# A hybrid SSD and attention encoder step on one core: order of the plain FFN tiles, low parts of three weight pairs by DMA, PSUM banks of the norms in the scan

## The chip, the cores and the metric

The kernel is one program on one core of one Trainium2 chip. The metric is the device time of that core in microseconds, the median of three runs: 2969.83 us before the change (2967.94 to 2970.08). The engines are named as in the profile: PE (TensorE, the matmuls), PEld (its weight loads), DVE (VectorE), ACT (ScalarE), POOL (GpSimd), SP (the queue that issues most DMAs). PSUM is the memory that matmuls write, in banks of 128 x 512 float32; SBUF is the memory that all other operands stand in.

## The reference

Two layers over 1024 prompt frames and 64 frames of a running stream, width 1024. Layer 0 is an SSD scan (Mamba-2) and a SwiGLU FFN, layer 1 band attention and a SwiGLU FFN; every sub-layer has a norm before and after it. Cut to what the change touches:

```python
def rmsnorm(x, w):
    return x * lax.rsqrt(jnp.mean(x * x, axis=-1, keepdims=True) + EPS) * w

def swiglu(u, w_in, w_out):
    g, up = jnp.split(u @ w_in, 2, axis=-1)
    return (jax.nn.silu(g) * up) @ w_out

def ssd_mixer(u, h0, conv_prev, w_in, ...):
    z, xbc, dt_raw = split(u @ w_in)
    xs, Bm, Cm = split(jax.nn.silu(conv(xbc)))
    dt = jax.nn.softplus(dt_raw + dt_bias)
    y, h_final = ssd_scan(xs, dt, A, Bm, Cm, h0)          # chunks of 64, a state per head
    y = (y + xs * D) * jax.nn.silu(z)
    yg = y.reshape(b, L, SSM_GROUPS, -1)
    yg = yg * lax.rsqrt(jnp.mean(yg * yg, -1, keepdims=True) + EPS)   # a norm per group
    return (yg * gnorm_w) @ w_out, h_final, new_conv
```

## The kernel before

**Matmuls in three products.** All inputs are float32. Each operand is kept as a high part (a cast to the PE's reduced float32) and a low part (the rest), and a product is the sum of high x high, high x low and low x high: `passes` (L446) issues these as lines 454, 455 and 456, `run_pair` (L1264) as 1280 to 1282. The third needs the low part of the weight.

**Weights.** The class `Weights` (L225) runs a plan of weight tiles of 128 x 1024 in a fixed order. `load` (L247) sends a tile by SP into a buffer of the ring `raw` (two buffers). `part` (L325) splits it into a tile of the ring `hl` (three buffers, `HLB`): ACT casts the high part (L340), DVE subtracts for the low part (L341); then the raw buffer is free and the next load can go out. A tile planned with `acc` is split otherwise: ACT casts (L334) and writes the negated high part into the low part's place (L335), the raw buffer is free, and POOL issues a DMA (L336) that reads the weight again from DRAM and adds it there. `get` hands out the next split weight, `put` returns the oldest one; each calls `advance`, which starts what the rings have room for.

**Ordering clock.** The order of PE's instructions is the order in which the program writes them. A class `Stream` (L90) keeps a clock of its own: matmuls add to it (3 n / 2360 for three products of n columns), and side tasks (generators that yield a cost and a delay) are resumed by `pump` when their delay is over and their condition holds, which happens in the middle and at the end of each unit. A unit (L461) is eight blocks of three products into one bank, with an evacuation. `wait_for` pushes the clock on without matmuls until a condition holds. The other engines' instructions are ordered at compile time by readiness and priority.

**Scan stage.** The projection's weights come as B, C, x of the first tile, over the three column slices `SL` of 384, 384 and 320, and then in the groups of `order` (L557): the first is x1 and z0 (tiles 17 and 0 of `w_in`), the next x2 and z1, and so on. `table_task` (L675) makes the tables of decays from dt: the matmuls `dtn`, after `TB_V` on the ordering clock `acsp` (L694), then `lastp` and `acT`, rows out to DRAM (`ascr`), and a flag that lets the SSD tasks start. `ssd_task` (L836) loads MT from `ascr`, transposes x (`xtp`), makes the states (`sp`), and for two blocks at a time `ssd_out` (L807) writes two tiles `yp` and two `yo`. Group norms are made by `rstd` (L482, tile `nst`: the sum of squares transposed, read by DVE at L498) and `bcast` (L513, tile `nbp`, read by ACT at L520).

**PSUM in the scan stage.** Eight banks: two of tag `mm` for units, two of tag `ax` (function `ax`, L436) that bnp, cbp, xtp, sp, nst, nbp and the tables share, and four of tag `yy` (pool `pyy`) for yp and yo.

**FFN entry.** `ffn_plan` (L1228) plans for each layer twelve plain weights (a gate and an up weight for tiles 0 to 5; `acc` for the first `NACC` = 3 tiles), then pairs of weights for `run_pair`, which computes a tile's gate and up halves by seven products of recombined operands (r0, ta, tb, b22: `pair`, L282, with sums on POOL and DVE). The plain tiles need the activations of one quarter at a time (256 columns); they cover the time in which the activations' sums are made for the pairs. `plain_pairs` (L1240) takes both weights of a tile, runs gate and up over quarter 0, then gate and up over quarter 1, and returns each weight after its unit of quarter 1. While the first tile runs, two more split buffers (`hx`) are there.

Of the kernel before, what the change touches and what calls it, by code (L numbers as in the profile page):

```python
# [16 lines left out]
P = 128  # L17
# [16 lines left out]
FT = 22  # L34
# [10 lines left out]
AT_W1, AT_W2 = 6.0, 2.5  # L45
SSD_GAP, SSD_D = 4.4, 8.0
ST_W, ST_RB = (6.5, 22.0, 22.0), (6.0, 1.0, 1.0)
TB_W, TB_V = 1.0, 14.0
ES = 0.5, 0.5, 0.0
OS = 1.9, 1.4  # L50
EP_W, ER_W, EQ_W = (9.4, 9.4, 2.2), (8.9, 8.9, 3.3), (11.0, 11.0)
# [1 line left out]
HIP = 3000  # L53
# [9 lines left out]
PGS = (0,), (1,), (2,), (3,), (4,), (5,)  # L63
NB0 = 6
BIG, TOP = 1e30, 3e38

NACC = 3
# [307 lines left out]
def hybrid_kernel(  # L375
# [4 lines left out]
    nc = tc.nc  # L380
    V, A, G, PE = nc.vector, nc.scalar, nc.gpsimd, nc.tensor
# [22 lines left out]
    for _ in range(17):  # L404
# [28 lines left out]
    def col(c):  # L433
        return pcs[:, c:c + 1]

    def ax(name):  # L436
        return pax.tile([P, 512], F32, tag="ax", name=name)

    def mm(name):
        return pmm.tile([P, 512], F32, tag="mm", name=name)  # L440
# [5 lines left out]
    def passes(ps, w, rhs, ks, n, parts=2, first=True, last=True):  # L446

        h, v = w["w"]
        nk = len(ks)
        cut = (nk + parts - 1) // parts  # L450
        for i, (kw, k) in enumerate(ks):
            h_, l_ = h[:, kw * P:(kw + 1) * P], v[:, kw * P:(kw + 1) * P]
            xh, xl = rhs(k)
            PE.matmul(ps[:, :n], h_, xh, start=(first and i == 0), stop=False)  # L454
            PE.matmul(ps[:, :n], h_, xl, start=False, stop=False)  # L455
            PE.matmul(ps[:, :n], l_, xh, start=False, stop=(last and i == nk - 1))  # L456
# [100 lines left out]
    order = []  # L557
# [8 lines left out]
            else:  # L566
                order.append((("x", 15), ("z", 14), ("z", 15)))
    W.plan(*[dict(src=[w_in[t]]) for t in (32, 36, 16)])
    for grp in order:
        W.plan(*[dict(src=[w_in[{"B": 32, "C": 36, "x": 16, "z": 0}[kd_] + i]]) for kd_, i in grp])  # L570

    MGS = ((0, 1, 2), (3, 4, 5), (6, 7))
    for b in range(2):
# [64 lines left out]
    with ExitStack() as es:  # L638
        pyy = es.enter_context(tc.tile_pool(reuse_waits="tile", name="pyy", bufs=4, space=PSUM))
# [336 lines left out]
        for s, (o, n) in enumerate(SL):  # L976
            xs = []
# [58 lines left out]
        first = [("B", 0), ("C", 0), ("x", 0)]  # L1036
        ws = [W.get(), W.get()]
# [3 lines left out]
        def scale_dt(s):  # L1041
            st.wait_for(lambda: s in done)
            ps = pend[s].pop(0)
            V.tensor_tensor(dtT[s][:64, :SL[s][1]], ps[:64, :SL[s][1]], rbs[s][:64, :SL[s][1]], op=ALU.mult)

        def finish(s):
            if s < 1:
                scale_dt(s)
            for e, ps in zip(ev, pend.pop(s)):
                e(s, ps)  # L1050

        for s in range(NSL):
            us, n = u[s], SL[s][1]
            pl, tg = pyy, "yy"
# [9 lines left out]
            for i in range(3):  # L1064
                ps = mm("mm") if i else pl.tile([P, 512], F32, tag=tg, name="mmp")
# [10 lines left out]
                dps = dt_unit(us, n, pl, tg)  # L1076
            pend[s] = [dps] * (s < 2) + box
        finish(2)
        for grp in order:
            ws = [W.get() for _ in grp]  # L1080
            ev = [evac_of(*f) for f in grp]
            if len(grp) < 3:
                seq = [(i, s) for s in range(NSL) for i in range(len(grp))]
                if grp is order[0]:

                    seq = [(0, 0), (0, 1), (1, 0), (1, 1), (1, 2), (0, 2)]
            else:
                seq = [(0, 0), (1, 0), (0, 1), (0, 2), (2, 0), (1, 1), (2, 1), (1, 2), (2, 2)]
            for i, s in seq:
                kd_, jj_ = grp[i]  # L1090
                q = 3 * jj_ + s
                if kd_ == "x":
                    st.wait_for(lambda: so["C"] > q - 5)
                elif kd_ == "z":
                    st.wait_for(lambda: so["D"] > q - 3)
                elif kd_ == "C" and q >= 5:
                    g_, s_ = divmod(q - 5, 3)
                    st.wait_for(lambda: so["C"] > 3 * (4 * g_ + 3) + s_)
                unit(ws[i], u[s], SL[s][1], lambda p_: ev[i](s, p_))
                if s == 2:  # L1100
                    W.put()
# [5 lines left out]
            ya[q] = [v4(R.get(), QS[q][1]) for _ in range(2)]  # L1107
        project((0, 1), uy[0], ya, None)
        st.wait_for(lambda: so["D"] == 3 * XT and len(rst_done) == NG * NSL)


    class Ops:
# [127 lines left out]
    def plain_pairs(ts, ops, hd, px, tmp):  # L1240

        n = ops.n
        ws = [(W.get(), W.get()) for t_ in ts]
        for q in range(2):
            st.wait_for(lambda: all(a_ in ops.plain for a_ in (f"a{q + 1}1", f"a{q + 1}2")))
            uq = ops.plain[f"a{q + 1}1"] + ops.plain[f"a{q + 1}2"]
            for t_, w2 in zip(ts, ws):
                x = tmp.tile([P, n], F32, tag=("p1", "u3")[q] + f"{t_ % 2}", name="x")

                def gate(ps):  # L1250
                    with tc.high_priority(HIP):
                        A.activation(x, ps[:, :n], AF.Silu)

                def mult(ps):
                    with tc.high_priority(HIP):
                        V.tensor_tensor(x, ps[:, :n], x, op=ALU.mult)
                    nc.sync.dma_start(hd[:, t_, q * n:(q + 1) * n], x)
# [248 lines left out]
    def start_ssd(ops, px, after, dn):  # L1506
# [29 lines left out]
    for b in range(2):  # L1536
        W.plan(*[dict(src=[w_o[m]]) for mg in MGS for m in mg])
    ffn_plan(1)
    done = done2
    uo = {}  # L1540
    with ExitStack() as es:
# [281 lines left out]
        for w in (wk, wv):  # L1823
            ps = mm("mm")
# [15 lines left out]
        for j in range(1, 8):  # L1840
# [3 lines left out]
            ws = [W.get(), W.get() if j > 1 else wv, W.get()]  # L1844
# [7 lines left out]
            while left:  # L1852
# [11 lines left out]
                s, i = now  # L1864
# [135 lines left out]
```

## Time and profile before

| | |
|---|---|
| median of three runs | 2969.83 us (2967.94 to 2970.08) |
| the profiled execution | 2970.8 us |
| its span, first to last instruction | 2969.1 us |
| mean granted clock | 0.996 |
| busy: DVE, ACT, POOL | 2037.2, 1394.6, 723.7 us |
| DMA | 363.35 MB, mean 122 GB/s |

Time is in us from the span's start. In a timeline a row is start, duration, engine, line, operation, output<-inputs, shape and count, and in brackets the idle time of the engine before it and the last event that ended it. That event can come from an engine which had finished long before, so a wait is read together with the rows of the other engines at that time. In a table of stretches the columns are the stretch, its length, then the busy time of PE, PEld, DVE, ACT and POOL with the number of instructions, the clock that was granted to PE as a share of full speed, the share of the DMA engines and their GB/s. The scan stage runs to about 715 us, the plain tiles of layer 0 from 868 to 937 us, those of layer 1 from 2217 to 2287 us.

### The profile page before, as it was taken

The page shows a single profiled execution, that of the slowest core. Times are in us where ns is not written, and L with a number is a line of the kernel's source. Part 1 is how long each engine was busy: PE and PEld are TensorE (multiplying, and loading weights), DVE is VectorE, ACT ScalarE, POOL GpSimd, SP SyncE. Part 2 cuts the span into 40 slices and gives each one's busy share as a digit, 9 for nine tenths or more (in the row PEclk, how much of TensorE's full clock was granted, in tenths as well). Part 3 has the DMA queues.
Part 4 walks back from the last instruction along what each step waited for, and adds up shares of the span by engine and source line. Part 5 has one row for each costly group of instructions (what it writes and reads, how often), then busy time and mean ns, then how long its engine had stood idle before and what let it go on. Part 6 is the DMA issues. An engine that isn't in the chain of part 4 may idle for free.

```text
span 2969.1 us, 56218 instructions
## 1 busy us (share of the span) xinstructions
PE 2916.9 (98%) x21562; PEld 2871.9 (97%) x21562; DVE 2037.2 (69%) x4455; ACT 1394.6 (47%) x2522; POOL 723.7 (24%) x877
## 2 busy tenths in 40 slices
PE   8999999999999999999999999999999999999999
PEld 7899999999999999999999899999899999999999
DVE  7887888785768555584557878778678645475544
ACT  6564645454454222244545666556653322244443
POOL 1333333331121343451111000000131333351111
PEclk9999999999999999999999999999999999999999
DMA  3333323234564222255655322223365222245654
GB/s 123 113 106 96 104 90 110 93 118 150 172 172 129 79 76 84 73 161 175 208 175 169 96 75 78 66 67 99 110 186 171 79 79 77 78 156 171 220 174 137
DMA packets 201550, 363.35 MB, mean 122 GB/s; under 512 B 20544, under 2 KB 149280, under 8 KB 201280
## 3 DMA queue, kind: packets, MB, share of 16 engines
q1 hardware_dynamic: 199488, 353.39, 38.3%
q0 software_dynamic: 1792, 6.36, 1.1%
q8 instruction: 169, 2.77, 0.4%
q14 instruction: 101, 0.83, 0.1%
HBM read 292.47 MB, written 62.74 MB: 120 GB/s over the span
## 4 chain that ended last, share of the span: by engine, by line
PE 85%; DVE 8%; DMA 3%; ACT 2%; issue 2%; POOL 0%; SPq 0%; DVEq 0%; ACTq 0%; POOLq 0%
PE px L1280 9%; PE px L1281 9%; PE px L1282 9%; PE mm L454 7%; PE mm L456 7%; PE mm L455 7%; PE po L1480 6%; PE po L1481 6%; PE po L1479 6%; PE mmx L455 3%; PE mmx L454 3%; PE mmx L456 3%; PE ptp L1712 2%; PE po L1747 2%; PE yp L816 1%
## 5 line engine op out<-in xcount | busy, mean ns | idle before, releaser
L454 PE MATMUL mm<-r,hl 128*128 128x384 f32 (+2 forms) x1664 | 555.1, 334 | 6.1 <-ACT BT L768 3.0
L456 PE MATMUL mm<-r,hl 128*128 128x384 f32 (+2 forms) x1664 | 539.6, 324 | 3.6 <-DVE hl L353 2.9
L455 PE MATMUL mm<-r,hl 128*128 128x384 f32 (+2 forms) x1664 | 538.2, 323 | 0.0
L341 DVE TENSOR_TENSOR hl<-raw,hl 128x1024 fp32r<-128x1024 f32 (+1 forms) x219 | 257.2, 1175 | 226.8 <-ACT hl L340 220.7
L1281 PE MATMUL px<-r,hl 128*128 128x288 f32 (+1 forms) x1184 | 347.3, 293 | 0.0
L454 PEld LDWEIGHTS mm<-r,hl 128*128 128x128 f32 x1664 | 315.4, 190 | 9.0 <-ACT BT L768 3.2
L456 PEld LDWEIGHTS mm<-r,hl 128*128 128x128 f32 x1664 | 314.5, 189 | 5.7 <-DVE hl L353 4.5
L455 PEld LDWEIGHTS mm<-r,hl 128*128 128x128 f32 x1664 | 315.3, 190 | 0.3
L1280 PE MATMUL px<-r,hl 128*128 128x288 f32 x1056 | 311.0, 294 | 0.0
L1282 PE MATMUL px<-r,hl 128*128 128x288 f32 x1056 | 310.7, 294 | 0.0
L340 ACT CAST hl<-raw 128x1024 fp32r<-128x1024 f32 (+1 forms) x219 | 220.0, 1005 | 175.3 <-PE po L1481 101.6
L480 POOL TENSOR_TENSOR ssum<-ssum,sq 128x256 f32<-128x256 f32 (+3 forms) x97 | 127.8, 1318 | 637.3 <-ACT sq L479 622.0
L1281 PEld LDWEIGHTS px<-r,hl 128*128 128x128 f32 x1184 | 222.3, 188 | 0.0
L1282 PE MATMUL px<-rx,hl 128*128 128x256 f32 x768 | 214.8, 280 | 6.7 <-DVE hl L341 6.7
L1280 PE MATMUL px<-rx,hl 128*128 128x256 f32 x768 | 215.3, 280 | 0.7 <-ACT hl L340 0.7
L1480 PE MATMUL po<-rx,hl 128*128 128x384 f32 (+1 forms) x624 | 201.7, 323 | 0.1
L1280 PEld LDWEIGHTS px<-r,hl 128*128 128x128 f32 x1056 | 198.4, 188 | 0.4 <-DVE u L1295 0.3
L1282 PEld LDWEIGHTS px<-r,hl 128*128 128x128 f32 x1056 | 198.3, 188 | 0.0
L1479 PE MATMUL po<-rx,hl 128*128 128x384 f32 (+1 forms) x608 | 197.3, 324 | 0.0
L1481 PE MATMUL po<-rx,hl 128*128 128x384 f32 (+1 forms) x608 | 196.5, 323 | 0.0
L1281 PE MATMUL px<-rx,hl 128*128 128x256 f32 x640 | 178.7, 279 | 0.0
L290 POOL TENSOR_TENSOR tt<-raw 128x512 f32<-128x512 f32 x40 | 54.7, 1367 | 438.6 <-DMA raw<-in_w_f_dram 308.9
(360 smaller groups left out, 8053.6 us busy)
## 6 DMA issues: line engine op xcount, KB each, us to landing
raw<-in_w_f_dram SPq DMA_DIRECT2D x154, 512.0 KB, 3.8
rx<-in_w_f_dram SPq DMA_DIRECT2D x54, 512.0 KB, 3.6
raw<-in_w_in_dram SPq DMA_DIRECT2D x40, 512.0 KB, 3.6
MT<-ascr SPq DMA_DIRECT2D x48, 384.0 KB, 4.3
sg<-hscr SPq DMA_DIRECT2D x88, 192.0 KB, 3.5
raw<-in_w_f_dram SPq DMA_DIRECT2D x44, 384.0 KB, 3.2
raw<-in_w_so_dram SPq DMA_DIRECT2D x32, 512.0 KB, 3.8
raw<-in_w_kv_dram SPq DMA_DIRECT2D x18, 512.0 KB, 3.5
```

Of the source, the lines that this page charges most:

```text
L340: self.nc.scalar.copy(h, v)
L341: (eng or self.eng or self.nc.vector).tensor_tensor(lo, v, h, op=ALU.subtract)
L454: PE.matmul(ps[:, :n], h_, xh, start=(first and i == 0), stop=False)
L455: PE.matmul(ps[:, :n], h_, xl, start=False, stop=False)
L456: PE.matmul(ps[:, :n], l_, xh, start=False, stop=(last and i == nk - 1))
L480: (eng or G).tensor_tensor(ssum[:, :n], ssum[:, :n], q[:, :n], op=ALU.add)
L1280: PE.matmul(ps, wh, ah[:, k, :], start=(k == 0), stop=False)
L1281: PE.matmul(ps, wh, al[:, k, :], start=False, stop=False)
L1282: PE.matmul(ps, wl, ah[:, k, :], start=False, stop=(k == 3))
L1479: PE.matmul(ps[:, :n], wh, xh, start=(k == 0), stop=False)
L1480: PE.matmul(ps[:, :n], wh, xl, start=False, stop=False)
L1481: PE.matmul(ps[:, :n], wl, xh, start=False, stop=(k == FT - 1))
```

## The change

Four edits. In the FFN entry the plain tiles after the first go weight by weight: gate over both quarters, then up over both, each weight taken when it is first used. The two weights of the last plain tile are planned with `acc`. In the scan, the weights of the first group (x1 and z0) are planned with `acc`, `nst` and `nbp` take a bank of tag `yy` from the first group to the end of the stage's projection, and `TB_V` is 10 instead of 14.

```diff
-TB_W, TB_V = 1.0, 14.0
+TB_W, TB_V = 1.0, 10.0
...
+    side = [None]
+
     def ax(name):
+        if side[0] and name in ("nst", "nbp"):
+            return side[0].tile([P, 512], F32, tag="yy", name=name)
         return pax.tile([P, 512], F32, tag="ax", name=name)
...
-    for grp in order:
-        W.plan(*[dict(src=[w_in[{"B": 32, "C": 36, "x": 16, "z": 0}[kd_] + i]]) for kd_, i in grp])
+    for g_, grp in enumerate(order):
+        W.plan(*[dict(src=[w_in[{"B": 32, "C": 36, "x": 16, "z": 0}[kd_] + i]], acc=g_ < 1) for kd_, i in grp])
...
         finish(2)
+        side[0] = pyy
         for grp in order:
...
         project((0, 1), uy[0], ya, None)
         st.wait_for(lambda: so["D"] == 3 * XT and len(rst_done) == NG * NSL)
+        side[0] = None
...
-        W.plan(*[dict(src=[w1[i]], acc=t_ < NACC) for t_ in range(NB0) for i in (t_, FT + t_)])
+        W.plan(*[dict(src=[w1[i]], acc=t_ < NACC or t_ == NB0 - 1) for t_ in range(NB0) for i in (t_, FT + t_)])
...
     def plain_pairs(ts, ops, hd, px, tmp):
 
         n = ops.n
-        ws = [(W.get(), W.get()) for t_ in ts]
-        for q in range(2):
+        first = ts == PGS[0]
+        xs, ws = {}, {}
+        for t_, i, q in [(t_, i, q) for t_ in ts for i, q in (((0, 0), (1, 0), (0, 1), (1, 1)) if first else ((0, 0), (0, 1), (1, 0), (1, 1)))]:
+            if (t_, i) not in ws:
+                ws[t_, i] = W.get()
             st.wait_for(lambda: all(a_ in ops.plain for a_ in (f"a{q + 1}1", f"a{q + 1}2")))
             uq = ops.plain[f"a{q + 1}1"] + ops.plain[f"a{q + 1}2"]
-            for t_, w2 in zip(ts, ws):
-                x = tmp.tile([P, n], F32, tag=("p1", "u3")[q] + f"{t_ % 2}", name="x")
+            if i == 0:
+                xs[t_, q] = tmp.tile([P, n], F32, tag=("p1", "u3")[q] + f"{t_ % 2}", name="x")
+            x = xs[t_, q]
...
-                for w, e in zip(w2, (gate, mult)):
-                    unit(w, uq, n, e, pl=px)
-                    if q:
-                        W.put()
+            unit(ws[t_, i], uq, n, mult if i else gate, pl=px)
+            if q:
+                W.put()
```

More of the change, by code (lines that the diff above doesn't have):

```diff
@@ L1242, in plain_pairs, with gate, mult @@
         n = ops.n
-        ws = [(W.get(), W.get()) for t_ in ts]
-        for q in range(2):
+        first = ts == PGS[0]
[3 more added lines that the diff above has]
+                ws[t_, i] = W.get()
             st.wait_for(lambda: all(a_ in ops.plain for a_ in (f"a{q + 1}1", f"a{q + 1}2")))
             uq = ops.plain[f"a{q + 1}1"] + ops.plain[f"a{q + 1}2"]
-            for t_, w2 in zip(ts, ws):
-                x = tmp.tile([P, n], F32, tag=("p1", "u3")[q] + f"{t_ % 2}", name="x")
[L1250 to L1257, printed above, removed]
-                for w, e in zip(w2, (gate, mult)):
-                    unit(w, uq, n, e, pl=px)
-                    if q:
-                        W.put()
+            if i == 0:
+                xs[t_, q] = tmp.tile([P, n], F32, tag=("p1", "u3")[q] + f"{t_ % 2}", name="x")
+            x = xs[t_, q]
+            def gate(ps):
+                with tc.high_priority(HIP):
+                    A.activation(x, ps[:, :n], AF.Silu)
+            def mult(ps):
+                with tc.high_priority(HIP):
+                    V.tensor_tensor(x, ps[:, :n], x, op=ALU.mult)
+                nc.sync.dma_start(hd[:, t_, q * n:(q + 1) * n], x)
+            unit(ws[t_, i], uq, n, mult if i else gate, pl=px)
+            if q:
+                W.put()
     def run_pair(t_, pr, bs, ends, ops, hd, px, tmp, apart=False):
```

## The prediction

> **What bounds the kernel now.** I read the page's totals first, then TensorE's waits, then a table of stretches around the longest waits, then the timelines there.
>
> ```profile
> PE 2916.9 (98%) x21562; PEld 2871.9 (97%) x21562; DVE 2037.2 (69%) x4455; ACT 1394.6 (47%) x2522; POOL 723.7 (24%) x877
> ```
>
> TensorE is busy for 2916.9 of 2969.1 us. The change removes no matmul, so it can win only the 52 us in which PE is idle, and time at a reduced clock. The waits of PE (who waited for whom: us in total, times, longest):
>
> ```profile
> PE px L1282 <- DVE hl L341: 6.7, 3, 2.6
> PE xtp L866 <- DVE nv L498: 4.8, 6, 0.8
> PE sp L885 <- POOL xe L877: 3.9, 1, 3.9
> PE sp L885 <- DVE xd L876: 1.2, 1, 1.2
> PE nbp L517 <- DVE hn L898: 0.7, 1, 0.7
> PE sp L885 <- ACT rb L520: 0.8, 1, 0.8
> ```
>
> The first row is the entry of the two FFNs, the others are in the scan stage. Idle time also costs clock. Stretches (us; busy of PE, PEld, DVE, ACT, POOL; granted clock; DMA):
>
> ```profile
> 937.40:941.50 4.10, 2.05 (x16) 1.65 (x14) 4.00 (x5) 3.21 (x4) 0.00 (x0) 1.00 0.77 236
> 941.50:944.90 3.40, 2.89 (x13) 2.89 (x14) 2.94 (x4) 2.48 (x3) 2.38 (x2) 0.50 0.21 72
> 101.80:108.60 6.80, 5.59 (x37) 4.75 (x36) 5.76 (x16) 2.00 (x3) 1.79 (x2) 0.50 0.01 3
> 671.80:675.20 3.40, 3.05 (x15) 3.05 (x16) 3.40 (x19) 1.46 (x5) 0.00 (x0) 0.51 0.53 170
> 2288.00:2291.00 3.00, 0.39 (x5) 0.20 (x3) 3.00 (x4) 0.00 (x0) 0.00 (x0) 1.00 0.75 216
> ```
>
> Behind an idle spell a stretch of 3.4 us (twice that in the third row) runs at a clock of 0.50, which costs half of its PE busy time: 2.89/2 = 1.45 us, 5.59/2 = 2.8 us, 3.05/2 = 1.5 us. The last row, 2.6 us of idle in layer 1, was followed by none, so a clock term may or may not come with a gap. The Trainium skill ("TensorE: Matmul & The Clock Gate", Part 1) has the clock fall only after a whole idle window of about 3.4 us. The trace disagrees: the first row has 2.05 us of PE work in 4.10 us, and the clock falls. By that rule the clock terms below would be zero and the gain would be 2.9 us less.
>
> **Part 1, FFN entry (both layers).** Six plain tiles run before the first recombined pair (run_pair at tile 6). Layer 0 (PE rows end with [idle before <- releaser]):
>
> ```profile
> 923.79 0.38 ACT L1252 ACTIVATE x<-mmx 128x256 f32<-128x256 f32 x1 [5.13 <-PE mmx L456]
> 924.07 1.04 ACT L340 CAST hl<-raw 128x1024 fp32r<-128x1024 f32 x1
> 929.31 0.38 ACT L1252 ACTIVATE x<-mmx 128x256 f32<-128x256 f32 x1 [0.61 <-PE mmx L456]
> 926.53 1.22 DVE L341 TENSOR_TENSOR hl<-raw,hl 128x1024 fp32r<-128x1024 f32 x1
> 927.77 0.33 SPq L252 DMA_DIRECT2D raw<-in_w_f_dram  x1
> 931.62 1.31 POOL L290 TENSOR_TENSOR tt<-raw 128x512 f32<-128x512 f32 x1 [47.30 <-DMA raw<-in_w_f_dram]
> 939.61 0.39 PE L1280 MATMUL px<-rx,hl 128*128 128x256 f32 x1 [0.66 <-ACT hl L340]
> 942.01 0.58 PE L1282 MATMUL px<-rx,hl 128*128 128x256 f32 x1 [1.90 <-DVE hl L341]
> 2290.96 0.39 PE L1282 MATMUL px<-rx,hl 128*128 128x256 f32 x1 [2.61 <-DVE hl L341]
> 2297.63 0.38 PE L1282 MATMUL px<-rx,hl 128*128 128x256 f32 x1 [2.17 <-DVE hl L341]
> 2291.32 0.62 ACT L340 CAST half<-raw 128x512 fp32r<-128x512 f32 x1 [4.95 <-DMA raw<-in_w_f_dram]
> ```
>
> The last plain weight is copied on ACT at 924.07, and its low part ends on DVE at 927.75. Only then is its raw buffer free and the last load of the first pair issued (927.77); POOL starts on it at 931.62, and PE stands for the pair's second operand twice, 0.66 for its high and 1.90 for its low part. With the clock term layer 0 loses 0.66 + 1.90 + 1.45 = 4.0 us, layer 1 2.61 + 2.17 = 4.8 us. The 2.17 are for the third operand, whose copy stood on ACT behind one for the next pair that waited for its load until 2291.32.
>
> The change moves this chain forward in two ways. First, a weight is now used for both quarters in a row and returned after two units. Two gate units of one quarter and the next lie two units apart, 923.79 to 929.31, so a unit takes 2.8 us. With three buffers the last weight is split when the gate weight before it ends, two units behind 915.25 (row below) and not three: 920.8 instead of 924.07. Second, with the low part by DMA the raw buffer is free when ACT has copied, 1 us later: the load goes out near 922 instead of 927.77, 6 us earlier, more than the 2.6 us that PE waits. The pair's second operand gets its buffer one unit sooner; the third as before, when the plain tiles end, but four products before PE asks for it, and the load that held up ACT in layer 1 comes forward with the rest. DVE loses two instructions of 1.22 us per layer; ACT gets two negations of 1.05. I book the removal in full: 8.8 us. What DVE still has to do there (splits of the activations) becomes late next, at the second half of the pair.
>
> Against it stands the time that such a DMA takes. The same operation exists in plain tiles 0 to 2 (source view of its line, all twelve; then the negation on ACT):
>
> ```profile
> DMA to landing us min/median/max: 6.2/8.7/10.4
> L335 ACT ACTIVATE hl<-hl x7: 1043/1046/1062, 855.4 to 2229.8; 128x1024 fp32r<-128x1024 f32 x7
> 915.25 1.06 ACT L340 CAST hl<-raw 128x1024 fp32r<-128x1024 f32 x1 [1.52 <-issue]
> ```
>
> The gate weight of the last tile is copied at 915.25, negated to 917.4, issued by POOL, and lands 6.2 to 10.4 us later: 923.6 to 927.8, by the median 926.1. Its low part is wanted four units behind 915.25, at 926.5. The up weight runs with the same margin, half a tile later. So the median is just in time and the slowest 1.3 us late; I take 0.3 us per layer, from 0 to 2.5 (both weights late). POOL has nothing behind these issues until the pair's subtractions. Part 1: 8.8 - 0.6 = **8.2 us**, bounds 3.8 and 8.8. The Trainium skill ("DMA: Bandwidth & Descriptors", Anatomy of one DMA) gives 2.0 us plus bytes at 436 GB/s for this queue, an estimate of 3.2 us for 512 KB; the trace's shortest is twice that, and by the page Part 1 would be 8.8.
>
> **Part 2, start of the scan.** Low parts of x1 and z0 by DMA, and the table's second step 10 instead of 14 after its first on the program's ordering clock:
>
> ```profile
> 60.54 1.05 ACT L340 CAST hl<-raw 128x1024 fp32r<-128x1024 f32 x1 [1.85 <-PE mmp L456]
> 70.38 0.22 DVE L721 TENSOR_TENSOR craw<-mm,rb 128x64 f32<-128x64 f32 x1
> 70.74 0.41 PE L454 MATMUL mm<-r,hl 128*128 128x384 f32 x1 [2.99 <-ACT BT L768]
> 72.05 0.45 DVE L691 TENSOR_TENSOR tt<-dt,negA 128x288 f32<-128x288 f32 x1
> 79.66 0.65 PE L694 MATMUL acsp<-tt,U 128*128 128x288 f32 x2
> 96.55 0.82 PE L866 MATMUL xtp<-ident,xsT 128*128 128x128 f32 x6
> 101.31 1.22 PE L885 MATMUL sp<-xe,Bn 128*128 128x128 f32 x6 [3.94 <-POOL xe L877]
> ```
>
> The 2.99 us wait before x1's first unit is for the bank that DVE empties at 70.38 (ACT is only the last event seen); two subtractions of 1.2 us stand ahead of it on DVE and go. But x1's low part now takes copy 61.6, negation 62.7, issue and 6.2 to 10.4 us: 69 to 73, middle 71.5. One wait is replaced by another: 70.74 becomes 71.5, a loss of **0.8 us** (gain of 1.7 to loss of 2.3). z0 is wanted two units later and is covered.
>
> The table's acsp stands on PE where the ordering clock puts it. After the first step the clock counts 1.63 + 3.25 + 3.25 for the rest of slice 2 and 1.95 for half of x1's first unit, 10.1 in all: due at 10.0, acsp now goes into the middle of that unit, not of the next one (79.66). That is near 74, 5 us earlier, and its input is ready at 72.05 + 0.45, so it does not wait. Everything from there to sp is a chain of data (table rows out, MT back, DVE, ACT, POOL), and from 96.55 PE has no units left until the first outputs are done: this is where it loses 3.94 + 1.21 us and 2.8 us of clock. Five microseconds earlier, the first sp finds its data. I leave 0.6 us for the second block's chain and count half the clock term: 5.15 - 0.6 + 1.4 = **6.0 us** (0 to 8).
>
> **Part 3, norms in the outputs' banks.** nst and nbp leave the two ax banks for the four yy banks.
>
> ```profile
> 242.35 0.49 PE L487 MATMUL nst<-ident,ssg 128*128 128x128 f32 x3
> 243.64 0.52 PE L866 MATMUL xtp<-ident,xsT 128*128 128x128 f32 x3 [0.80 <-DVE nv L498]
> 660.72 0.39 PE L517 MATMUL nbp<-ident,rst 128*128 128x128 f32 x2
> 661.33 0.60 DVE L830 SCALAR_TENSOR_TENSOR y<-xsT,pcs,yp 128x384 f32<-128x384 f32 x1
> 670.21 0.47 DVE L933 TENSOR_TENSOR ssg<-ssg,sq 128x320 f32<-128x320 f32 x1
> 670.83 0.52 PE L487 MATMUL nst<-ident,ssg 128*128 128x128 f32 x3 [2.69 <-DVE nv L499]
> 672.15 0.48 PE L517 MATMUL nbp<-ident,rst 128*128 128x128 f32 x1 [0.80 <-DVE nv L498]
> ```
>
> xtp waits 0.80 us, six times, until DVE has read nst out of the shared pair of banks: 4.8 us, gone. At the end of the scan the same sharing costs 0.76, 0.73 and 0.80: 2.3 us. The 2.69 us are not bank time: ssg is finished at 670.68 on DVE, and PE starts right behind. What it costs: at 660.72 all four yy banks are just written, and nbp has to wait for L830 at 661.33 + 0.60, about 1.2 us, and the nst behind it for the next reader, about 1 us. PE then comes to the 2.69 us wait 2.2 us later, which hides it; without that cover Part 3 would be 2.2 us less. **7.1 us**, bounds 3 and 8.6 (with the clock term of 1.5).
>
> **Sum.** 8.2 - 0.8 + 6.0 + 7.1 = 20.5 us. The profiled execution took 2970.8 us (span 2969.1 and 1.7 around it), so 2950.3; the median of the runs, 2969.83, is 1 us lower: **2949.3 us**. Its own range, from the bounds: 8.8 + 1.7 + 8 + 8.6 = 27 us to 3.8 - 2.3 + 0 + 3 = 4.5 us gained; not all bad ends come together, so 2942 to 2962.
>
> **Rivals.** *The table gains nothing*: the waits before sp re-form one block later, because DVE, busy 5.76 of 6.80 us there, or the arrival of MT is the limit and not acsp. For it: DVE's share in that stretch; against: 22 us of pure chain hang on acsp. 20.5 - 6.0 = 14.5: 2955.3 us.
>
> *The low parts land late*: all at 10.4 us. Then Part 1 gives 3.8, x1 loses 2.3 and the table, with PE later, half of its 6.0: with 7.1 these are 11.6 us, 2958 us. For it: half of the twelve took over 8.7 us. Against it: the longest came where several were under way at once, and the new ones go out two units apart.
>
> *Starved issues*: the low parts now go out where DVE has no pause, unlike most of tiles 0 to 2. If a landing took half as long again as the longest, 15 us, the gate weight would land at 932.4 and be 5.9 us late in each layer, x1 6.2 us later than booked: 20.5 - 2 x 5.6 - 6.2 = 3 us, 2967 us. Against it: the twelve stay within 6.2 to 10.4. The Trainium skill ("SBUF — State Buffer", Who interferes with whom) says that DVE in a two-port mode keeps GpSimd from writing descriptors, but it excepts tensor_tensor; no run so far shows the starving.
>
> *Slower: the output banks become the bottleneck.* Twelve nst and some seven nbp groups go into banks of which each output step needs all four. If each costs what the two at 660.72 cost, 2.2 us (half where it enters, half at the next output step that finds a bank still held), and no later wait hides it, 19 x 2.2 = 42 us are lost against 20.5 gained: 2991 us. It decides from 20.5/19 = 1.1 us each. Against it: at 242.35 the last outputs are ten microseconds old, and only a few of the nineteen follow outputs directly.
>
> **Numbers.** Forecast 0.55, table 0.14, late landing 0.12, starved 0.06, banks 0.13. 2942 to 2966 us holds the first three but for their tails, 0.8. A measurement of this kernel tells some 0.2%, 6 us, from no change: faster (below 2964) is 0.55 + 0.14 + most of 0.12, 0.79; the same is the starved case and a rest, 0.08; slower the banks, 0.13.
>
> **What would show it.** In the new trace: no wait of px for hl (or under 0.7 us) and 1.00 for the clock behind tile 5 in both layers; the weight load near 922; DMA landings of 6 to 10 us for four more issues per kernel and two in the scan; acsp near 74 and the wait for xe gone; no xtp wait for nv; a wait of about 1 us of nbp behind an output step at 660. Wrong would be a wait of mmx L456 for the landing of a low part above 1.5 us, a wait of yp or nst for y above 1 us many times, or a wait for xe that has merely moved.

## The result, and the profile after

After the change the median is 2951.22 us (four runs, 2950.43 to 2954.82) against 2969.57 us for the kernel before on the same chip: a ratio of 0.9942, 95% interval 0.9924 to 0.9959, 18.35 us or 0.6% faster. The forecast was 2949.3 us in a range of 2942 to 2966. The total came out, but not by the terms that were booked: one of the three parts gave nothing, the two others gave more than booked. The first line of the profile after, busy time and share of each engine:

```profile
PE 2911.7 (99%) x21562; PEld 2870.6 (97%) x21562; DVE 2024.9 (69%) x4449; ACT 1399.2 (47%) x2528; POOL 729.8 (25%) x883
```

The number of matmuls is the same. PE's busy time is 5 us less (fewer stretches at half clock, fewer matmuls behind a wait), and the rest of the gain is idle time that went. To see where, both traces are cut at the same instructions of PE, so that each stretch holds the same work. Table of stretches of the kernel before (stretch, length, busy time of PE, PEld, DVE, ACT, POOL with their instructions, granted clock, DMA share, GB/s): start of the scan, rest of the scan, FFN entry of layer 0, FFN entry of layer 1, and a piece of the scan with two waits of xtp for nv.

```profile
48.84:185.38 136.54, 128.26 (x884) 124.11 (x884) 113.11 (x277) 76.15 (x116) 45.19 (x73) 0.95 0.35 105
185.38:714.31 528.93, 518.20 (x3715) 506.88 (x3714) 419.44 (x1070) 269.11 (x431) 174.63 (x284) 1.00 0.33 103
903.18:963.27 60.09, 57.27 (x468) 56.67 (x467) 50.89 (x81) 22.89 (x32) 11.76 (x9) 0.97 0.37 112
2251.83:2312.86 61.03, 56.25 (x471) 55.85 (x469) 52.73 (x83) 25.04 (x35) 11.58 (x9) 1.00 0.40 120
376.52:441.04 64.52, 62.85 (x437) 61.37 (x436) 50.45 (x143) 28.29 (x47) 23.52 (x37) 1.00 0.29 90
```

The same five of the kernel after:

```profile
47.29:174.60 127.31, 124.56 (x883) 120.34 (x883) 110.96 (x278) 77.15 (x118) 47.19 (x75) 0.99 0.41 121
174.60:692.85 518.25, 515.23 (x3715) 506.98 (x3715) 417.58 (x1070) 269.32 (x432) 173.08 (x284) 1.00 0.34 105
881.81:942.82 61.01, 57.40 (x468) 56.97 (x467) 47.39 (x80) 24.91 (x34) 14.20 (x11) 0.97 0.45 126
2232.44:2292.74 60.30, 57.80 (x470) 57.20 (x469) 51.01 (x82) 25.71 (x36) 14.15 (x11) 0.97 0.50 138
362.33:424.56 62.23, 62.23 (x438) 61.33 (x436) 50.53 (x144) 28.82 (x47) 23.48 (x38) 1.00 0.29 93
```

The start of the scan is 9.23 us shorter (booked: 5.2), the rest of the scan 10.68 (booked: 7.1), the FFN entry 0.92 longer in layer 0 and 0.73 shorter in layer 1 (booked: 8.2 shorter in all). Ahead of the first cut lie 1.55 us more, from a stretch of clock 0.50 at 43.8 that the profiled execution of before had and that of after had not; the kernels run later have it or not, without an edit there. The stretches between the cuts and behind the last add 1.3 us the other way.

**Start of the scan, after** (timeline; the landing line is from the view of the source line that issues the accumulating DMAs, all 18 of them):

```profile
63.96 0.22 DVE L725 TENSOR_TENSOR craw<-mm,rb 128x64 f32<-128x64 f32 x1
68.51 0.65 PE L698 MATMUL acsp<-tt,U 128*128 128x288 f32 x2
94.00 0.52 PE L870 MATMUL xtp<-ident,xsT 128*128 128x128 f32 x3 [1.32 <-DVE xd L880]
95.09 0.91 PE L889 MATMUL sp<-xe,Bn 128*128 128x128 f32 x6 [0.57 <-DVE hn L902]
DMA to landing us min/median/max: 5.2/8.0/10.5
```

DVE empties the bank at 63.96 instead of 70.38 (1.55 us of that lie ahead of the stage): two subtractions that stood ahead of it are gone, and a third comes behind it (67.78 instead of 68.87). The low part of x1 was the fastest of all those DMAs, 5.2 us. x1's first unit no longer waits in front (2.99 us before); inside it PE stands 0.13 us for the landing of the low part. acsp stands in the middle of that unit and so came 11.15 us earlier, 9.6 of it within the stage, where 5 were forecast. The two waits of sp, for xe (3.94) and for xd (1.21), are gone, and so are the 6.8 us at half clock; a wait of xtp of 1.32 (ended by DVE's xd) and one of sp of 0.57 (ended by DVE's hn) stand there instead.

**Rest of the scan.** No xtp waits for nv any more, as forecast. The last rows of the two tables show what two such waits were worth: 64.52 - 62.23 = 2.29 us, so 1.14 each, though the brackets said 0.80. PE's busy time fell too (62.85 to 62.23), because the first matmuls behind a wait take longer in the record (0.36 and 0.39 us behind the two waits of the FFN entry below, against 0.28 for those that follow). Cut once more at the same instruction near 600 us, the scan up to there, which holds all six waits, went from 414.66 to 406.67 us, and the end of the scan from 114.27 to 111.58. In e1 below, where this part is not edited, the two took 413.69 and 114.41, so the six waits were worth 7 to 8 us and the end 2.7 to 2.8. At the end of the scan one new wait stands:

```profile
643.24 0.51 PE L521 MATMUL nbp<-ident,rst 128*128 128x128 f32 x2 [3.02 <-DVE y L834]
```

That is the wait of nbp for an output bank which was forecast at about 1 us, here 3.02 with 3.4 us of half clock behind it; the 0.76, 0.73, 2.69 and 0.80 us that stood in this region are gone.

**FFN entry.** The waits of PE, after (who waited for whom: us in total, times, longest):

```profile
PE px L1291 <- DVE hl L341: 3.6, 2, 1.8
...
PE px L1289 <- DVE x L1266: 1.8, 1, 1.8
```

Layer 0 there (timeline of SP, POOL, DVE, ACT and PE):

```profile
901.11 0.33 SPq L252 DMA_DIRECT2D raw<-in_w_f_dram  x1
904.97 1.80 POOL L290 TENSOR_TENSOR tt<-raw 128x512 f32<-128x512 f32 x1 [1.66 <-DMA raw<-in_w_f_dram]
916.45 1.21 DVE L341 TENSOR_TENSOR hl<-tt,hl 128x1024 fp32r<-128x1024 f32 x1
917.92 2.12 DVE L1160 TENSOR_TENSOR r<-r 128x1152 fp32r<-128x1152 f32 x1
921.25 0.69 DVE L308 TENSOR_TENSOR tt<-tt,raw 128x512 f32<-128x512 f32 x1 [1.21 <-POOL tt L290]
921.86 1.35 DVE L1160 TENSOR_TENSOR r<-r 128x1152 fp32r<-128x1152 f32 x1
924.73 1.22 DVE L341 TENSOR_TENSOR hl<-tt,hl 128x1024 fp32r<-128x1024 f32 x1
916.53 2.30 POOL L341 TENSOR_TENSOR half<-raw,half 128x512 fp32r<-128x512 f32 x1 [6.76 <-ACT half L340]
918.78 2.44 POOL L290 TENSOR_TENSOR tt<-raw 128x512 f32<-128x512 f32 x1
921.14 1.04 ACT L340 CAST hl<-tt 128x1024 fp32r<-128x1024 f32 x1
923.69 0.36 PE L1289 MATMUL px<-rx,hl 128*128 128x256 f32 x1 [1.78 <-DVE x L1266]
926.00 0.39 PE L1291 MATMUL px<-rx,hl 128*128 128x256 f32 x1 [1.84 <-DVE hl L341]
```

The load of the first pair goes out at 901.11; with the 21.4 us by which this trace is ahead there that is 922.5, as forecast, and POOL starts on it 5.3 us earlier than before. The second operand (ta, 916.45) is in time. But PE now waits for the third (tb, 924.73), and before that for a bank that DVE empties. Between ta and tb stand splits of activations for the second half of the pair (L1160) and a sum for the next pair (L308), and DVE goes slowly: one split takes 2.12 us and the next 1.35, and at 921.25 it has waited 1.21 us for POOL. The operand that was 1.90 us late is no longer late; the one behind it is, by as much.

In layer 1 it is still the second operand that is late: PE stands for it at 2270.54 for 1.75 us (2.61 before), and the wait for the third (2.17 before) is gone. There (timeline of ACT, POOL and DVE):

```profile
2266.40 0.62 ACT L340 CAST half<-raw 128x512 fp32r<-128x512 f32 x1 [7.23 <-DMA raw<-in_w_f_dram]
2267.09 2.31 POOL L341 TENSOR_TENSOR half<-raw,half 128x512 fp32r<-128x512 f32 x1 [7.41 <-ACT half L340]
2268.27 2.21 DVE L341 TENSOR_TENSOR hl<-tt,hl 128x1024 fp32r<-128x1024 f32 x1
```

The load that held up ACT came 5.5 us earlier, as forecast, but now the copy of ta stands behind it, and ta's low part takes 2.21 us beside POOL where it took 1.21 in layer 0. In both layers the clock was 0.50 for 3.4 us behind these waits, where 1.00 was forecast.

### The profile page after: what moved, and what is told of

The parts are those of the page before. It is cut to its first block, busy times and chain, and to the rows that moved or that the text cites. A ratio compares the mean times of both kernels' runs of the same rounds, so it can differ in the third digit from the quotient of the medians.

```text
span 2949.1 us, 56250 instructions
## 1 busy us (share of the span) xinstructions
PE 2911.7 (99%) x21562; PEld 2870.6 (97%) x21562; DVE 2024.9 (69%) x4449; ACT 1399.2 (47%) x2528; POOL 729.8 (25%) x883
## 4 chain that ended last, share of the span: by engine, by line
PE 87%; DVE 6%; DMA 3%; ACT 2%; issue 1%; POOL 0%; SPq 0%; DVEq 0%; ACTq 0%; POOLq 0%
PE px L1289 9%; PE px L1290 9%; PE px L1291 9%; PE mm L460 7%; PE mm L458 7%; PE mm L459 7%; PE po L1489 6%; PE po L1490 6%; PE po L1488 6%; PE mmx L459 3%; PE mmx L458 3%; PE mmx L460 3%; PE ptp L1721 2%; PE po L1756 2%; PE S L1690 1%
## 5 line engine op out<-in xcount | busy, mean ns | idle before, releaser
L341 DVE TENSOR_TENSOR hl<-raw,hl 128x1024 fp32r<-128x1024 f32 (+1 forms) x213 | 249.8, 1173 | 218.9 <-ACT hl L340 216.7
L340 ACT CAST hl<-raw 128x1024 fp32r<-128x1024 f32 (+1 forms) x213 | 213.8, 1004 | 161.2 <-PE po L1490 100.3
L1291 PEld LDWEIGHTS px<-rx,hl 128*128 128x128 f32 x768 | 146.2, 190 | 4.2 <-DVE hl L341 4.0
```

Of the source, the lines that this page charges most:

```text
L340: self.nc.scalar.copy(h, v)
L341: (eng or self.eng or self.nc.vector).tensor_tensor(lo, v, h, op=ALU.subtract)
L1291: PE.matmul(ps, wl, ah[:, k, :], start=False, stop=(k == 3))
```

## The experiments

Each is timed against the kernel before in the same session, five rounds; the ratio stands with its 95% interval. Stage lengths are those of the tables above, cut at the same instructions.

### One part at a time, on the kernel before

**e1_table: the table's second step alone.**

```diff
-TB_W, TB_V = 1.0, 14.0
+TB_W, TB_V = 1.0, 10.0
```

> Before, with the table's second step due at 10 instead of 14; nothing else. Prediction: acsp goes out some 5 us earlier, the waits for xe and xd (3.94 + 1.21 us) and half the clock term behind them go: 6.0 us, 2963.8. Reading of the trace after: the same place, but acsp follows x1's first unit and not the clock alone; 6 to 8 us, and x1's first unit stays where it was, 70.7. Rival (the table gains nothing, DVE or the arrival of MT is the limit): within 1 us of before.

The run took 2966.17 us, ratio 0.9984 (0.9975 to 0.9992), 4.3 us faster by the medians. acsp and the first block's sp, and the stretch of the start:

```profile
74.71 1.07 PE L694 MATMUL acsp<-tt,U 128*128 128x288 f32 x2
97.86 0.83 PE L885 MATMUL sp<-xe,Bn 128*128 128x128 f32 x6
100.17 0.91 PE L885 MATMUL sp<-xe,Bn 128*128 128x128 f32 x6 [0.64 <-DVE hn L898]
```

acsp went to 74.71 (forecast: near 74), the first sp no longer waits, no half clock follows, and the stage took 130.42 us against 136.54: 6.1, where 6.0 were booked. Of these, 3.75 are idle time of PE and 2.4 its busy time at half clock. The rival that acsp was not the limit is out.

**e2_low: low parts of x1 and z0 by DMA alone.**

```diff
-    for grp in order:
+    for g_, grp in enumerate(order):
-        W.plan(*[dict(src=[w_in[...]]) for kd_, i in grp])
+        W.plan(*[dict(src=[w_in[...]], acc=g_ < 1) for kd_, i in grp])
```

> Before, with the low parts of x1 and z0 by an accumulating DMA; nothing else. Prediction: one wait replaces another, 0.8 us slower (1.7 faster to 2.3 slower). Reading of the trace after: it is 3 to 5 us faster, since x1's low part landed 5.2 us behind its issue (not 6.2 to 10.4) and the 2.99 us wait in front of x1's first unit goes with the clock stretch behind it (another 1.7); the waits for xe and xd stay.

The run took 2968.19 us, ratio 0.9990 (0.9981 to 0.9999), 2.3 us faster by the medians, not slower. The wait for the landing (timeline of PE):

```profile
69.37 0.44 PE L456 MATMUL mm<-r,hl 128*128 128x384 f32 x1 [1.34 <-DMA hl<-in_w_in_dram]
```

It replaces the 2.99 us, so 1.65 us of waiting are gone. The stage fell by 3.4 us, since the stretch of half clock behind the wait went as well. But in e6, where this stage is unedited, that stretch was absent behind the same 2.99 us, and the stage was as short (e2, then e6):

```profile
48.76:181.87 133.11, 126.79 (x883) 122.72 (x883) 110.84 (x275) 77.87 (x118) 46.35 (x75) 0.96 0.41 116
48.16:181.09 132.93, 125.17 (x884) 121.10 (x884) 113.14 (x278) 76.13 (x116) 45.07 (x73) 0.97 0.36 108
```

In the other kernels with this stage unedited (before, e3, e4, e5) it took 135.7 to 137.0 us. So the wait's 1.65 us are this edit's, and the rest of the 3.4 is the clock's, which can go without it.

**e3_banks: norms in the outputs' banks alone.** The diff is the change's: `side`, its use in `ax`, and where it is set and cleared.

```diff
+        if side[0] and name in ("nst", "nbp"):
+            return side[0].tile([P, 512], F32, tag="yy", name=name)
```

> Before, with the norms in the outputs' banks; nothing else. Prediction: 7.1 us, of it 0.80 for each of six waits of xtp. Reading of the trace after: each of the six costs 1.14 us and not 0.80 (the matmuls behind a wait restart the pipeline), 6.9 us, and 2.7 at the end of the scan: 9.5 to 10 us, 2960. Rival (output banks the bottleneck): slower than before, 2971 to 3011.

The run took 2962.10 us, ratio 0.9971 (0.9959 to 0.9982), 8.35 us faster by the medians; the rest of the scan fell from 528.93 to 518.43, by 10.5 us. The rival with the output banks as the bottleneck is out: twelve nst and the nbp cost one wait of 3.02 us.

**e4_entry: both edits of the FFN entry alone** (the hunks of `ffn_plan` and `plain_pairs`).

```diff
+acc=t_ < NACC or t_ == NB0 - 1
...
+((0, 0), (0, 1), (1, 0), (1, 1))
```

> Before, with both edits of the FFN entry (plain tiles weight by weight, low parts of the last tile by DMA); nothing else. Prediction: 8.2 us faster, no wait of px for hl above 0.7 us. Reading of the trace after: within 1 us of before; px waits 1.8 + 1.8 us in layer 0 and 1.8 + 0.8 in layer 1 for DVE's low parts and a bank that DVE empties, with a stretch of clock 0.50 in both layers.

The run took 2971.36 us, ratio 1.0004 (0.9995 to 1.0013): no gain. Layer 0 took 62.01 us (60.09 before), layer 1 60.29 (61.03). The waits are those of the kernel after: 1.76 for the bank and 1.81 for the third operand in layer 0, 1.83 for the second in layer 1.

**e5_order and e6_acc: the two edits of the entry, each alone.**

```diff
# e5_order
+((0, 0), (0, 1), (1, 0), (1, 1))
# e6_acc
+acc=t_ < NACC or t_ == NB0 - 1
```

> Before, with the plain tiles weight by weight alone; low parts of the last tile stay on DVE. Prediction: the last weight is split 3.3 us earlier and with it the pair's chain, so most of the 2.6 us (layer 0) and 4.8 us (layer 1) of waits go: 4 to 8 us faster. Rival (DVE's own queue is the limit, not the load): nothing is taken off DVE, so within 1 us of before, with waits of px for hl of some 1.8 us left in both layers.

> Before, with the low parts of the last plain tile by DMA alone; order of the units as before. Prediction: the load goes out 2.7 us earlier, just the 2.6 us that PE waits: 4 to 8 us faster. Rival (DVE's queue is the limit): DVE loses two instructions of 1.22 us per layer, so the waits shrink by at most that, 0 to 2 us faster in all, and a wait for a low part on DVE is left.

e5 took 2973.80 us, 1.0009 (1.0000 to 1.0018), with entries of 62.00 and 61.80 us. e6 took 2971.70 us, 1.0001 (0.9992 to 1.0010), with entries of 62.71 and 60.34. Where PE waits in the last plain tile of layer 0, e5 first (timeline of PE, one row of each kernel):

```profile
933.24 0.50 PE L456 MATMUL mmx<-rx,hl 128*128 128x256 f32 x1 [2.09 <-DVE hl L341]
```

```profile
927.93 0.58 PE L456 MATMUL mmx<-rx,hl 128*128 128x256 f32 x1 [3.52 <-DMA hl<-in_w_f_dram]
```

Neither expectation of a gain holds. With the order alone DVE is late with the last plain tile's low part (2.09) and again with the pair's (2.59). With the DMA alone the pair's waits shrink to 0.69 us, but the DMA of the up weight goes out 3.6 us later in the entry than in the new order and lands 3.52 us late (2.85 in layer 1). The two edits need each other: the order gives the DMA the time to land. Together they remove both waits in layer 0 and leave the third operand and the bank in front of it; in layer 1 they leave the second operand.

### What limits the FFN entry

**e8_half1: one buffer for the b22 part.** In layer 1 of the kernel after, ACT waited 7.23 us at the next pair's b22 copy, with the copy of ta behind it.

```diff
-W.half.pool, W.half.bufs = W.tt.pool, 2
+W.half.pool, W.half.bufs = W.tt.pool, 1
```

> After, with one buffer instead of two for the b22 part, so that the second pair's copy cannot stand on ACT in front of the first pair's second and third operand. If that copy (which waits 7.2 us for its load in layer 1) is what makes ta late there, the 1.75 us wait of px in layer 1 and its clock stretch go, layer 0 keeps its 1.8 + 1.8 (DVE's queue): 1.5 to 3 us faster than after. Rival (DVE's splits of the activations alone set the end in both layers): no difference.

The run took 2985.03 us, 1.0054 (1.0041 to 1.0066): 34 us slower than after, against both the expectation and its rival. The entry itself got a little shorter, 59.73 and 59.94 us, so ACT's blocking was worth some 1.3 and 0.4 us and no more. In layer 0 the wait for the third operand stayed at 1.84; in layer 1 the 1.75 us for the second went, and 0.65 for the bank and 1.83 for the third came in their place. The loss is in the loop of pairs behind it (table of stretches, the same work in both, the kernel after first):

```profile
942.82:1323.76 380.94, 380.94 (x3025) 380.94 (x3024) 222.47 (x378) 129.36 (x216) 156.14 (x132) 1.00 0.31 97
```

```profile
944.32:1344.74 400.42, 388.44 (x3026) 384.93 (x3024) 229.15 (x375) 125.92 (x213) 151.29 (x133) 0.99 0.30 93
```

There PE of the kernel after never stands, and with one buffer it stands in most pairs.

**e10_poolsum and e11_poolboth: work moved from DVE to POOL.**

```diff
# both: the second pair's two sums (the lines that count the pairs in it["no"] are left out)
-v = self.nc.vector.tensor_tensor
+v = (self.nc.gpsimd if it["no"] == 1 else self.nc.vector).tensor_tensor
# e11 also: two of the seven splits of the second quarter pair
+GS = "s3", "s4"
...
-V.tensor_tensor(l_, L[nm_], h, op=ALU.subtract)
+(G if ops.b and nm_ in GS else V).tensor_tensor(l_, L[nm_], h, op=ALU.subtract)
```

> After, with the two sums of the second pair on POOL instead of DVE, in both layers. If DVE's queue is what makes the first pair's third operand late (1.21 us of waiting for POOL and 0.69 of L308 stand in front of it in layer 0), the wait of px for the bank (1.78) goes and the wait for hl shrinks: 2 to 3.5 us faster than after, 2948 to 2949. Rival (the end is set by ACT's copies or by the loads): no difference, within 0.7 us.

> After, with the second pair's sums and two of the seven splits (s3, s4) of the second quarter pair on POOL, in both layers. By DVE's queue as the limit two more instructions of 1.27 us leave it in front of the third operand: the waits of px for hl go, 3 to 7 us faster than after, unless POOL, at 1.3 us and more for half the width, becomes late for the second half of the pair (a wait of px for r or for tt some 10 us later), which would eat it.

The runs took 2956.38 us (0.9952, 0.9939 to 0.9964) and 2957.06 us (0.9953, 0.9940 to 0.9965). Both expectations were of a gain over after; by the medians both runs are 5 to 6 us slower than it (the intervals overlap), though DVE had fewer instructions to do. The entries took 61.25 and 61.49 us in e10 and 60.94 and 64.70 in e11, against 61.01 and 60.30. So in the profiled execution of e10 only 1.4 of 5.7 us lie in the entries; the others lie in stages that the edit leaves as they are, and their cause was not looked for. The number of instructions in DVE's queue is not the limit. What the rows of e11 show, DVE first and then POOL (timeline):

```profile
915.76 3.67 DVE L345 TENSOR_TENSOR hl<-tt,hl 128x1024 fp32r<-128x1024 f32 x1
914.67 3.67 POOL L1164 TENSOR_TENSOR r<-r 128x1152 fp32r<-128x1152 f32 x1 [4.37 <-DVE r L1164]
```

The low part of ta, 1.21 us elsewhere, took 3.67: POOL's instruction ends at 918.34, and DVE's 1.09 us after it. In the rows of the kernel after it is the same: POOL's L341 ends at 916.53 + 2.30 = 918.83, DVE's split at 917.92 + 2.12 = 920.04, 1.21 later; POOL's L290, started at 918.78, ends at 921.22, 1.18 behind DVE's split (it takes 1.31 alone). The two engines take turns, instruction by instruction. DVE's instructions that read one operand from PSUM took no longer beside POOL (x<-mmx,x at 917.59 in the kernel after, 0.41 us as elsewhere). The Trainium skill ("SBUF — State Buffer", Who interferes with whom) states this: a DVE instruction with two SBUF inputs contends with a GpSimd instruction that reads SBUF, and the one that comes first holds the shared ports for its whole length. The trace agrees to some 0.15 us: behind POOL, DVE's instructions needed 1.09 and 1.21 us for their own 1.21 and 1.35.

**e12_dvepair: the opposite, the second pair's POOL work moved to DVE** (the counter is left out again).

```diff
-g = self.nc.gpsimd.tensor_tensor
+g = (self.nc.vector if it["no"] == 1 else self.nc.gpsimd).tensor_tensor
...
-self.part(it, "b22", self.half, b22, self.nc.gpsimd)
+self.part(it, "b22", self.half, b22, self.nc.vector if it["no"] == 1 else self.nc.gpsimd)
```

> After, with the second pair's work on POOL (two subtractions of 512 columns and the low part of b22) moved to DVE, in both layers: the opposite of the two runs before. If POOL's instructions slow DVE's while both run (a split of 1.27 us took 2.12 beside POOL in layer 0, the low part of ta 2.21 instead of 1.21 in layer 1, and DVE waited 1.21 for POOL's difference), the three cost DVE some 2.0 us and save it 2 to 3.5: splits fall to 1.27 to 1.35, the low part of tb comes 1 to 2 us earlier, 2 to 4 us faster than after, 2947 to 2949. Rival (the number of instructions on DVE is the limit): 1 to 2.5 us later in each layer, 2 to 5 us slower than after.

The run took 2946.04 us, 0.9923 (0.9909 to 0.9936): the fastest of all, 5.2 us below after by the medians (of two sessions, whose kernels before are 0.07 us apart; the intervals still overlap, and the stages below decide). That is as expected from the contention, and against the rival. DVE in layer 0 and PE's remaining wait (timeline), then the entries of both layers (table of stretches):

```profile
916.67 0.68 DVE L344 TENSOR_TENSOR half<-raw,half 128x512 fp32r<-128x512 f32 x1
917.61 1.34 DVE L1163 TENSOR_TENSOR r<-r 128x1152 fp32r<-128x1152 f32 x1
918.88 0.68 DVE L293 TENSOR_TENSOR tt<-raw 128x512 f32<-128x512 f32 x1
921.68 1.21 DVE L344 TENSOR_TENSOR hl<-tt,hl 128x1024 fp32r<-128x1024 f32 x1
922.95 0.39 PE L1294 MATMUL px<-rx,hl 128*128 128x256 f32 x1 [1.17 <-DVE hl L344]
```

```profile
880.67:938.19 57.52, 56.04 (x468) 55.47 (x467) 47.35 (x83) 24.80 (x34) 7.56 (x8) 1.00 0.48 137
2230.38:2288.28 57.90, 55.98 (x470) 55.53 (x469) 48.59 (x80) 25.24 (x34) 9.00 (x7) 1.00 0.51 134
```

With three more instructions DVE's busy time in layer 0 is the same, 47.35 against 47.39, because what it loses in work it had lost in waiting for POOL's turn: what POOL did in 2.30 and 2.44 us takes DVE 0.68 each. The split is back at 1.34, and DVE no longer waits 1.21 us for POOL's difference. The wait for the bank fell from 1.78 to 0.23, that for the third operand from 1.84 to 1.17, and the clock stays at 1.00. The entries are 3.5 and 2.4 us shorter than after's, 2.6 and 3.1 shorter than before's: 5.7 of the 8.2 us that were booked. One thing else changed in layer 0: three splits of the activations stood between ta and tb, now two do, and the third comes behind tb. Of the 2.1 us by which tb's low part moved closer to ta's, that is 1.3, so the turns alone are not separated from it there. In layer 1 no split changed sides; there ta's low part took 1.22 us instead of 2.21 and the first split 1.35 instead of 2.36.

### The scan by itself

**e9_scan: the three scan edits, entry as before.**

```diff
# against the kernel after
-acc=t_ < NACC or t_ == NB0 - 1
+acc=t_ < NACC
```

(and `plain_pairs` of before).

> Before with the three scan edits (table, low parts of x1 and z0, norms' banks) and the FFN entry as before. If the parts simply add, as measured one by one (4.3 + 2.3 + 8.35), 15 us faster than before, 2956, and the other 4 us of the whole change need the FFN entry. If the two edits at the start of the scan help each other (the table's acsp follows x1's first unit, and that follows its low part), 18 to 20 us faster, 2950 to 2953, as fast as the whole change. Prediction's sum without its 8.2 for the entry: 12.3 us.

The run took 2952.64 us, 0.9940 (0.9926 to 0.9953): the whole gain without the entry. Its scan took 127.40 + 518.52 us, the kernel after's 127.31 + 518.25. By stages the parts add: 6.1 + 3.4 against 9.1 at the start. By whole runs, 4.3 + 2.3 + 8.35 = 15 against 17.9, they don't; the intervals of the small ones (2 to 3 us to each side) are wide enough for that, and no other cause was looked for.

**e7_nst_only: nbp back in the two ax banks, nst in the outputs' banks.**

```diff
-        if side[0] and name in ("nst", "nbp"):
+        if side[0] and name == "nst":
```

> After, with nbp back in the two ax banks and only nst in the outputs' banks. If the 3.02 us wait of nbp for y at 643 and the clock stretch behind it (1.5 us) are the price of nbp's place, they go: 3 to 4.5 us faster than after, 2947 to 2948. Prediction's account (2.2 us of new waits there, hidden by the 2.69 us wait that follows): the old 0.73, 2.69 and 0.80 us waits come back in their place, 1 to 3 us slower than after.

The run took 2951.51 us, 0.9938 (0.9925 to 0.9950): neither was right. The 3.02 us wait and its clock stretch go, and waits of 0.75, 0.72, 0.87 and 0.96 us come in their place; the rest of the scan takes 518.23 us, the kernel after's 518.25. For nbp the two places cost the same.

## Why the prediction's total was right and a part of it wrong

**FFN entry (booked 8.2, found 0).** The first steps hold: the load near 922, the low parts of the last tile landing 6.3 to 7.0 us behind their issue without a wait of PE (0.3 per layer were booked, nothing came). The step that failed is "I book the removal in full", with what is late next put at the second half of the pair. In layer 0 it was late in the first half: the third operand, three products behind the old wait, by 1.84 us, with a bank in front of it, by 1.78. In layer 1 the second operand stayed late, by 1.75. Over the kernels with and without both edits, the entry of layer 0 takes 61.0 to 62.2 us with them and 60.1 to 61.3 without, that of layer 1 60.3 and 60.9 to 61.1. What the prediction had not asked is how long DVE's instructions would take with POOL's work for the next pair, now early too, beside them. The trace of before showed it already: a split that took 1.35 us in one place took 2.46 beside POOL at 934 (timeline of before):

```profile
934.18 1.75 POOL L341 TENSOR_TENSOR half<-raw,half 128x512 fp32r<-128x512 f32 x1
934.69 2.46 DVE L1154 TENSOR_TENSOR r<-r 128x1152 fp32r<-128x1152 f32 x1
```

e11 and e12 show it from both sides, the second with the change of order in layer 0 that is told there. The clock term of 1.45 us was no price of its own either: in e9, whose entry is that of before, no stretch of half clock came, and layer 0 took as long (60.22 us against 60.09), since PE came earlier to the next wait and stood longer:

```profile
884.11:944.33 60.22, 56.20 (x469) 55.40 (x466) 51.36 (x82) 23.20 (x34) 11.81 (x9) 1.00 0.39 115
```

**x1's low part (booked 0.8 lost, found 1.65 won, up to 3.4 with the clock).** The mis-sized term is the landing: 6.2 to 10.4 us was the range of the twelve in the FFN, and x1's took 5.2 to 6.1 us in all eight kernels that have it. Why it is faster stays open. That few others of its kind were under way (one, z0's) does not explain it: two of the twelve had none beside them and took 7.1 and 8.8 us. The clock term behind the 2.99 us was not booked at all.

**Table (booked 6.0, found 6.1 alone).** Right in place, mechanism and size, though within it the idle time gave 3.75 us where 4.55 were booked, and the clock 2.4 where 1.4 were. acsp stood at 68.51 in the whole change rather than 74 because x1's first unit, in which it stands, came earlier and not later.

**Norms' banks (booked 7.1, found 10.5).** Right in mechanism. The mis-sized term is the wait itself: 0.80 us in the bracket cost 1.14 in the piece with two of them, which makes 6.9 for six and not 4.8; the whole part that holds the six gave 8.0 (7.0 against e1). The end of the scan gave 2.7, where 2.3 were booked: the price of nbp's new place was as booked in kind and larger in size (3.02 with a clock stretch), and what it replaced larger still.

**The sum and the rivals.** 8.2 us were booked too much; 2.4 to 4.2 for x1, 3.4 for the banks and the first clock stretch of 1.55 were not booked. The total came out because these errors have opposite signs, and that is luck. Of the rivals, late or starved landings are out (5.2 to 7.3 us for the six new ones), so is the table without effect (e1), and the output banks did not become a bottleneck (e3).

## What to carry to other kernels

A chain that is pulled forward has a next operand with a deadline of its own: follow it to the end of the work that is due together, with the durations that the instructions have beside their new neighbours, before booking a removed wait in full. When DVE is late, look at what POOL does at that time: moving work to the idle POOL can make DVE slower, and taking work off POOL can be worth more than its price on DVE. Price a PE wait by stretches cut at the same instructions, not by the bracket, and compare a stage with its unedited runs before its clock is put down to an edit.

## What the runs showed of the hardware that was not expected

DVE and POOL with operands in SBUF took strict turns: 1.21 to 1.35 us became 2.1 to 3.7 us beside POOL, 1.31 became 2.44 beside DVE, each ending one full instruction behind the other. Two PE waits of 0.80 us cost 2.29 us together.

The stretch of half clock behind a wait is no fixed price: 2.99 us were followed by one in the kernel before and in e1, e3, e4 and e5 and not in e6, with the same instructions there. The granted-clock records of the fourteen traces show what decides it. In each trace all such stretches start on one grid of 3.41 us: in the kernel before at 43.8, 57.4, 71.1 and 101.8, which are 4, 4 and 9 steps apart. Counted from 30 us on, every one of the 63 steps at full clock in which PE was busy for less than 45% was followed by a stretch. Between 45% and 56% some were; above that none was, except at one place, behind a step near 54 us in nine traces that holds the matmuls dtn (18 small ones, 64x32), which the record counts as busy. The 2.99 us wait left its step 12% to 40% busy in the five kernels with a stretch, and 49% in e6: it straddled two steps there. So the same wait costs clock or not by where it falls on the grid, and the grid stood differently in each execution.

An accumulating DMA of 512 KB landed within 5.2 to 10.5 us of its issue in one kernel. The slowest had three others of its kind under way, but two with none took 6.7 and 8.2 us, so what sets the time stays open.
